# Hybrid mLSTM and DeltaNet layer on one core: which buffers hold the split keys and queries, and which engine transposes and scales in the first segment

## The chip, the core and the metric

The kernel runs on one core of a Trainium2 chip. A core has five engines with an instruction stream of their own, which wait for one another through semaphores: TensorE (PE, matrix products into PSUM), VectorE (DVE), ScalarE (ACT), GpSimd (POOL) and SyncE (SP), whose queue issues nearly all DMAs here. The metric is the device time of one execution in microseconds (us); lower is better.

## The reference, cut to what matters

One layer: an input norm, one joint projection, two families of heads (4 mLSTM heads with 128 key and 256 value columns, 8 gated DeltaNet heads with 128 and 128), a gate on each, an output projection, a final norm. The sequence has 2048 tokens of 1024 columns, all in fp32.

```python
h = rms_norm(x, attn_norm)
mq, mk, mv, mo, mz, mi, mf, gqkv, gz, gb, ga = split(h @ w_in)
# mLSTM, per chunk: D = decay matrix, P = exp(D - m) * (q k^T)
num = w_inter * (q C) + P v
C = decay * C + (ws * k)^T v                  # ws: a weight per token
# gated DeltaNet, per chunk:
a_mat = I + strict_lower((beta k) k^T * gamma)
U, W = triangular_solve(a_mat, [beta v, beta k e^g])
v_new = U - W S ; o = q e^g S + tril(q k^T * gamma) v_new ; S = e^g_last S + k'^T v_new
x = x + concat(y_m, y_g) @ w_out ; out = rms_norm(x, final_norm)
```

## The kernel before

The 2048 tokens are cut into 4 segments of 512; in a segment a chunk is 128 tokens, so each step has 4 chunks. A segment runs eight windows: P0 M0 P1 M1 P2 M2 P3 M3 (in the last segment M2 and M3 stand behind P3). Window P*n* projects DeltaNet pair *n* (two heads, j = 0 and 1): columns `gq`, `gk`, `gv`, `gz`. Window M*n* projects mLSTM head *n*: `mq`, `mk`, `mv`, `mo`, `mz`. Each fp32 product is made of three products of fp32r parts (`hh`, `hl` of the activations, `whi`, `wlo` of the weights). After the segments comes the output projection, from about 1905 us.

Between the projections' matmuls stand the matmuls of the recurrences. The order of TensorE's instructions is written out (`manual_schedule`); the other engines are ordered by a scheduler's own timeline and `high_priority`, and each runs its instructions strictly in its list's order. Work of a pair or head runs in the windows behind its projection: the gate rows and decay matrices of pair *n* in window M*n*, the triangular solve and the chain of products in the next P and M windows, the mLSTM chunks of head *n* in window P*n+1*.

What the change touches:

- **First segment (`raw[0]`).** Here x is projected before it is normalised, because the norm's factor `rbc0` is not ready, and the weights are split on the fly by ACT (L179) and POOL (L182). `fm_out` (L375) therefore multiplies each projected tile by `rbc0` on DVE as it copies it from PSUM: `mq`, `mk`, `xingk` and so on.
- **Keys of an mLSTM head by token.** `mk` comes with tokens along the columns; the state's update needs them along the partitions (`kw`). The table `MT` says for each of three kinds of segment (first, middle two, last) and head which engine transposes: 1 is DVE, 16 transposes of 32x128 (L504, called from L590); 0 is TensorE, four 128x128 transposes by `ident` into a PSUM tile `ktp` (L601), with a copy scaled by `ws` on DVE (L603). Heads marked in `MF` ("fast") make two fp32r parts of `ws*kw` instead, `kws_pt` (ACT, L609) and `kws_nm` (DVE, L610). In the first segment heads 0 to 2 are fast, head 3 is not; its `kw` is scaled by POOL (L595).
- **Split keys and queries of a pair.** `split_kq(j)` (L789) makes `kh` (ACT) and `kl` (DVE and POOL, L804) of head j; the products `kk` (L821 to L823) read them in the order j = 0 then 1, two chunks each. The tiles are borrowed: j = 0 takes two tiles of tag `xk` (which the segment's x rows `xt` and `load_h` also use), j = 1 takes `lbt` (the tile that later holds the solve's matrix, and in other windows the gate rows' `ew` and the split `pts`) and the tiles `pt` and `nm`. There is one tile each of `lbt`, `pt` and `nm`.
- **What uses `nm` next.** The decay rows of the following mLSTM head are loaded into `nm` by a DMA (L561). DVE makes `ptt` from it (L565), ACT its exponential (L567). Behind that ACT copies `mk` (L371, later segments), DVE transposes it into `kw`, and then takes the value tile `vlo` out of PSUM (L537 in the first segment, L540 later). Projections go into three PSUM tiles `pj`, so TensorE stops at a product `pt_mv` (L363) when `vlo` is three tiles late.
- **The solve of a pair.** `ua` (L832) goes to memory and comes back as `lbt` (L841, L845); 31 steps of `tb` and `xb` (L850, L854) follow on DVE, then DMAs `e_d` and `E`, then `dmz` (L904, L905), for which the products `zp` (L910) wait on TensorE.
- **End of a segment.** `rms_stats` of the next one loads its four `xt` tiles (L131), ACT squares them (L132), DVE makes `rs` (L133), POOL its power (L137) and DVE `dg` (L140). `load_h` makes `hl` (L342) of four row tiles, the last of which stands in `lbt`, so it waits for the end of pair 3's solve; the first products of the next segment, `pt_gz` (L363 to L365), need it.

Of the kernel before, what the change touches and what calls it, by code (L numbers as in the profile page):

```python
# [10 lines left out]
F32 = mybir.dt.float32  # L11
F32R = mybir.dt.float32r
AF = mybir.ActivationFunctionType
ALU = mybir.AluOpType
# [3 lines left out]
P = 128  # L18
# [3 lines left out]
NCH = T // P  # L22
# [12 lines left out]
MW, MPR, VPR = ((0.07, 0.85), 200, 200)  # L35
# [20 lines left out]
VT = ((0, 0, 0, 0), (1, 1, 1, 1), (1, 0, 0, 0))  # L56
KTR = ((0, 0, 0, 0), (1, 1, 1, 1), (0, 1, 0, 0))
QT = ((1, 1, 1, 1), (1, 1, 1, 1), (1, 1, 0, 1))
MT = ((1, 1, 1, 1), (1, 1, 1, 1), (1, 1, 1, 0))
KF = ((0, 1, 1, 1), (1, 1, 1, 1), (1, 1, 1, 0))  # L60
MF = ((1, 1, 1, 0), (1, 1, 1, 0), (1, 0, 0, 0))
KE = ('vector', 'gpsimd')
# [7 lines left out]
def hybrid_layer(  # L70
# [16 lines left out]
    nc = tc.nc  # L87
# [14 lines left out]
    sm = wstack.enter_context(tc.tile_pool(name="sm", bufs=2, side="right"))  # L102
    cl = wstack.enter_context(tc.tile_pool(name="cl", bufs=2, side="right"))
    wkp = ctx.enter_context(tc.tile_pool(name="wkp", bufs=1, side="left"))
# [86 lines left out]
    for seg in range(NSEG):  # L191
        for kind, n in ORDER_LAST if seg == NSEG - 1 else ORDER:
            for i in range(4) if kind == "M" else (3, 1, 0, 2) if n == 0 else (1, 0, 2, 3):
                nm, key = f"{kind}{seg}_{n}_{i}", (kind, n, i)
# [40 lines left out]
    rbc0 = cst.tile([P, T], F32, name="rbc0")  # L235
# [131 lines left out]
    def fm_out(dst, ps, scale=None):  # L367

        if not raw[0]:
            if scale is None:  # L370
                nc.scalar.copy(dst, ps)  # L371
            else:
                nc.scalar.activation(dst, ps, AF.Copy, scale=scale)
        elif scale is None:
            nc.vector.tensor_tensor(dst, ps, rbc0, op=ALU.mult)  # L375
        else:
            nc.vector.scalar_tensor_tensor(dst, ps, scale, rbc0, op0=ALU.mult, op1=ALU.mult)

    def tm_done(ps, t, done, scaled=True):
        if raw[0] and scaled:  # L380
# [115 lines left out]
    def by_dve(which, seg, pr):  # L496
        return which[2 if seg == NSEG - 1 else min(seg, 1)][pr]

    def to_tokens(src, dst):

        s4 = src.rearrange("p (c a j) -> p c a j", c=NCH, a=4)
        for a in range(4):
            for b in range(4):
                nc.vector.transpose(dst[32 * a:32 * a + 32, :, 32 * b:32 * b + 32],  # L504
                                    s4[32 * b:32 * b + 32, :, a, :])


    def m_proj(seg, n, r):
# [46 lines left out]
    def m_chunks(seg, h, r, st):  # L555
        s_ = f"{seg}_{h}"
# [3 lines left out]
        nm = wk.tile([P, T], F32, tag="nm", name=f"nm{s_}")  # L560
        nc.sync.dma_start(nm, st["rows"][h, :].partition_broadcast(P))  # L561
        pt = wk.tile([P, T], F32, tag="pt", name=f"ptt{s_}")
# [14 lines left out]
        fast = by_dve(MF, seg, h)  # L577
# [10 lines left out]
            ps2 = split(pt, "pts", wkp, "lbt", nc.vector)  # L588
            qw2 = split(qw, "qws", sm, "xk", nc.gpsimd, bufs=XKB)
        yield  # L590
        kw = sm.tile([P, NCH, P], F32, tag="kw", name=f"kw{s_}", bufs=1)
        if fast or by_dve(MT, seg, h):
            to_tokens(kT, kw)
            if not fast:
                nc.gpsimd.tensor_tensor(  # L595
                    kw, kw, ws[:, :, h:h + 1].broadcast_to([P, NCH, P]), op=ALU.mult)
        else:
            ktp = psc.tile([P, 512], F32, tag="cp", name=f"ktp{s_}")
            for c in range(NCH):
                cs = slice(c * P, (c + 1) * P)  # L600
                nc.tensor.transpose(ktp[:, cs], kT[:, cs], ident)  # L601
            for c in range(NCH):
                nc.vector.tensor_scalar_mul(  # L603
                    kw[:, c, :], ktp[:, c * P:(c + 1) * P], ws[:, c, h:h + 1])
        if fast:
            kw2 = [wk.tile([P, NCH, P], F32R, tag=tag, name=f"kws{s_}_{tag}") for tag in ("pt", "nm")]
            for c in range(NCH):
# [4 lines left out]
                    op0=ALU.mult, op1=ALU.subtract)  # L612
# [124 lines left out]
    def g_prep(seg, pr, r, st):  # L737
        s_ = f"{seg}_{pr}"
# [9 lines left out]
        for j in range(2):  # L748
# [4 lines left out]
            for c in range(NCH):  # L753
                nc.vector.scalar_tensor_tensor(
                    ua_[:, c, 1, :], gbc[:, c * P:(c + 1) * P], gcol[:, c, h0 + j:h0 + j + 1],
                    negmask, op0=ALU.subtract, op1=ALU.min)
# [31 lines left out]

        def split_kq(j):  # L789

            kh = (wkp.tile([P, NCH, 2, P], F32R, tag="lbt", name=f"kh{s_}_{j}") if j else
                  sm.tile([P, NCH, 2, P], F32R, tag="xk", name=f"kh{s_}_{j}", bufs=XKB))
            if j:
                kl = [wk.tile([P, 2, 2, P], F32R, tag=tag, name=f"kl{s_}_{j}_{tag}")
                      for tag in ("pt", "nm")]
            else:
                kl_ = sm.tile([P, NCH, 2, P], F32R, tag="xk", name=f"kl{s_}_{j}", bufs=XKB)
                kl = [kl_[:, 0:2], kl_[:, 2:4]]
            for i, f in enumerate((kT[j], qT[j])):
                f = f.rearrange("p (c t) -> p c t", c=NCH)  # L800
                nc.scalar.copy(kh[:, :, i, :], f)
                for c2 in range(2):
                    cs = slice(c2 * 2, c2 * 2 + 2)
                    getattr(nc, KE[i]).tensor_tensor(  # L804
                        kl[c2][:, :, i, :], f[:, cs], kh[:, cs, i, :].bitcast(F32),
                        op=ALU.subtract)
            return kh, kl

        fast = by_dve(KF, seg, pr)
        kqs = [split_kq(j) for j in range(2)] if fast else None  # L810
        l_d = dpool.tile([2 * NCH, 4, 1024], F32, tag="l_d", name=f"l_d{s_}")
        for j in range(2):
            ua_ = ua[j]
            for c2 in range(NCH // 2):
                kp = psc.tile([P, 512], F32, tag="cp", name=f"kk{s_}_{j}_{c2}").rearrange(
                    "p (a b c) -> p a b c", a=2, b=2)
                for a in range(2):
                    if fast:
                        kh, kl = kqs[j]
# [10 lines left out]
                for a in range(2):  # L830
                    c = c2 * 2 + a
# [6 lines left out]
        lbt = wkp.tile([P, 32, 32], F32, tag="lbt", name=f"lbt{s_}")  # L838
# [43 lines left out]
        if by_dve(QT, seg, pr):  # L882
# [3 lines left out]
            for a in range(4):  # L886
# [4 lines left out]
                                op0=ALU.mult, op1=ALU.add)  # L891
# [209 lines left out]
    for seg in range(NSEG):  # L1101
# [17 lines left out]
        for kind, n in ORDER_LAST if last else ORDER:  # L1119
# [27 lines left out]
            else:  # L1147
# [256 lines left out]
```

## Time and profile before

| what | value |
|---|---|
| runs, us | 2284.42, 2275.52, 2281.76; median 2281.76 |
| the profiled execution | 2285.25 us, its span 2283.5 us |
| TensorE (PE) | busy 2210.1 us, 97% of the span, 14798 matmuls |
| VectorE (DVE) | busy 1842.6 us, 81% |
| ScalarE (ACT), GpSimd (POOL) | 38%, 35% |
| chain that ended last | PE 62%, DVE 25%, DMA 5%, ACT 4% |
| mean granted TensorE clock | 0.985 of full speed |

The span is what the trace covers; the execution's own time is 1.75 us longer. Busy times overlap, so they don't add up to the span. The chain is followed back from the last instruction, at each step to what released it; an engine's share of it says how often the end hung on that engine.

### The profile page before, as it was taken

How to read it: one execution, taken by the hardware profiler on the slowest of the kernel's cores; microseconds unless marked ns; L12 is line 12 of the kernel's file. 1: busy time of each engine (PE TensorE's matmuls, PEld its weight loads, DVE VectorE, ACT ScalarE, POOL GpSimd, SP SyncE). 2: the span in 40 equal slices, each digit the busy share in tenths (PEclk: the TensorE clock that was granted, in tenths of full speed). 3: DMA queues.
4: the chain of work that ended last, by engine and by line, in shares of the span. 5: the costliest groups of instructions: out<-in, count | busy, mean ns of one | idle time of the engine just before them, and what ended most of it. 6: DMA issues, size and time to landing. Idle time of an engine off the chain costs nothing.

```text
span 2283.5 us, 41793 instructions
## 1 busy us (share of the span) xinstructions
PE 2210.1 (97%) x14798; PEld 1963.8 (86%) x14798; DVE 1842.6 (81%) x5168; ACT 861.8 (38%) x2289; POOL 797.3 (35%) x1220
## 2 busy tenths in 40 slices
PE   8899999989999999999999999999999999999998
PEld 7779898987989898988898989898988997788787
DVE  7988888788897979888979798788757737878784
ACT  5445454535343434352424243524244334111111
POOL 4657565652120202521212114212111115555543
PEclk9999999999999999999999999999999999999999
DMA  8767676764536464655454546544546545222321
GB/s 273 265 236 252 231 242 240 255 216 157 193 135 213 138 212 159 224 167 182 162 187 163 176 169 237 178 152 166 184 168 209 192 152 162 80 96 92 102 84 65
DMA packets 183322, 409.19 MB, mean 179 GB/s; under 512 B 51736, under 2 KB 84632, under 8 KB 183112
## 3 DMA queue, kind: packets, MB, share of 16 engines
q1 hardware_dynamic: 182392, 405.74, 52.4%
q8 instruction: 116, 1.90, 0.3%
q14 instruction: 94, 0.77, 0.1%
q10 hardware_dynamic: 720, 0.79, 0.1%
HBM read 309.68 MB, written 96.90 MB: 178 GB/s over the span
## 4 chain that ended last, share of the span: by engine, by line
PE 62%; DVE 25%; DMA 5%; ACT 4%; issue 2%; POOL 2%; SPq 0%; POOLq 0%; ACTq 0%; DVEq 0%
PE po L1260 5%; PE po L1259 5%; PE po L1258 5%; DVE tb L850 3%; DVE xb L854 3%; DVE kw L504 2%; PE pf_gv L355 2%; PE pf_gv L353 2%; PE pf_gv L354 2%; PE pt_gz L365 2%; PE pf_gq L353 2%; PE pt_gz L363 2%; PE pt_gz L364 2%; PE pt_mo L363 2%; PE pt_mo L364 2%
## 5 line engine op out<-in xcount | busy, mean ns | idle before, releaser
L1219 DVE STREAM_TRANSPOSE ytt<-yl 32x256 f32<-32x256 f32 x448 | 195.3, 436 | 45.3 <-POOL ylo L1187 39.2
L1016 POOL TENSOR_TENSOR gms<-gms,nhalf 128x2 f32<-128x2 f32 x64 | 46.7, 729 | 395.8 <-DVE gms L1014 386.5
L850 DVE TENSOR_TENSOR tb<-xb,lbt 128x248 f32<-128x248 f32 (+30 forms) x496 | 170.1, 343 | 17.8 <-DMA lbt<-l_d 5.0
L854 DVE TENSOR_TENSOR xb<-xb,tb 128x248 f32<-128x248 f32 (+30 forms) x496 | 167.7, 338 | 13.2
L363 PE MATMUL pt_mv<-whi_M,hh 128*128 128x256 f32 x512 | 152.7, 298 | 21.7 <-DVE vlo L540 14.6
L363 PE MATMUL pt_mz<-whi_M,hh 128*128 128x256 f32 x512 | 149.7, 292 | 7.6 <-DVE tz L550 7.5
L363 PE MATMUL pt_gz<-whi_P,hh 128*128 128x256 f32 (+1 forms) x512 | 149.7, 292 | 1.8 <-ACT whi_P L179 1.5
L364 PE MATMUL pt_mv<-wlo_M,hh 128*128 128x256 f32 x512 | 148.6, 290 | 0.1
L365 PE MATMUL pt_mv<-whi_M,hl 128*128 128x256 f32 x512 | 148.5, 290 | 0.0
L363 PE MATMUL pt_mo<-whi_M,hh 128*128 128x256 f32 x512 | 148.4, 290 | 0.0
L365 PE MATMUL pt_gz<-whi_P,hl 128*128 128x256 f32 (+1 forms) x512 | 146.7, 286 | 0.4 <-DVE hl L342 0.2
L364 PE MATMUL pt_gz<-wlo_P,hh 128*128 128x256 f32 (+1 forms) x512 | 146.4, 286 | 0.4 <-DVE wlo_P L182 0.4
L365 PE MATMUL pt_mz<-whi_M,hl 128*128 128x256 f32 x512 | 145.1, 283 | 0.0
L364 PE MATMUL pt_mz<-wlo_M,hh 128*128 128x256 f32 x512 | 145.1, 283 | 0.0
L364 PE MATMUL pt_mo<-wlo_M,hh 128*128 128x256 f32 x512 | 144.2, 282 | 0.0
L365 PE MATMUL pt_mo<-whi_M,hl 128*128 128x256 f32 x512 | 144.2, 282 | 0.0
L363 PEld LDWEIGHTS pt_mv<-whi_M,hh 128*128 128x128 f32 x512 | 101.4, 198 | 25.1 <-DVE vlo L540 16.0
L1267 ACT ACTIVATE jkf<-xr 128x512 f32<-128x512 f32 (+1 forms) x33 | 20.4, 619 | 271.5 <-DVE xr L1265 148.4
L1258 PE MATMUL po<-woh,yh 128*128 128x512 f32 (+1 forms) x297 | 114.6, 386 | 1.5 <-ACT yh L1185 1.5
L1260 PE MATMUL po<-woh,ylo 128*128 128x512 f32 (+1 forms) x297 | 114.9, 387 | 0.1
L1259 PE MATMUL po<-wol,yh 128*128 128x512 f32 (+1 forms) x297 | 114.3, 385 | 0.0
L182 POOL TENSOR_TENSOR wlo_M<-wraw_M,whi_M 128x256 fp32r<-128x256 f32 x128 | 98.4, 801 | 40.6 <-ACT whi_M L179 40.6
(407 smaller groups left out, 7541.7 us busy)
## 6 DMA issues: line engine op xcount, KB each, us to landing
whi_M<-wdM SPq DMA_DIRECT2D x96, 512.0 KB, 4.0
wlo_M<-wdM SPq DMA_DIRECT2D x96, 512.0 KB, 5.5
whi_P<-wdP SPq DMA_DIRECT2D x90, 512.0 KB, 4.7
wlo_P<-wdP SPq DMA_DIRECT2D x90, 512.0 KB, 6.0
wraw_M<-in_wg_dram SPq DMA_DIRECT2D x32, 512.0 KB, 5.8
wdM<-whi_M SPq DMA_DIRECT2D x32, 512.0 KB, 2.9
wdM<-wlo_M SPq DMA_DIRECT2D x32, 512.0 KB, 5.0
wraw_P<-in_wg_dram SPq DMA_DIRECT2D x30, 512.0 KB, 5.7
```

The lines of the kernel that those rows point to most:

```text
L182: eng.tensor_tensor(lo[:, ks, :], raw_[:, ks, :], hi[:, ks, :].bitcast(F32), op=ALU.subtract)
L353: nc.tensor.matmul(ps, lhsT=hi[k // HK][:, k % HK, c0:c0 + P], rhs=hh[k], start=(k == 0), stop=False)
L363: nc.tensor.matmul(ps, lhsT=hh[k][:, ts], rhs=hi, start=(k == 0), stop=False)
L364: nc.tensor.matmul(ps, lhsT=hh[k][:, ts], rhs=lo, start=False, stop=False)
L365: nc.tensor.matmul(ps, lhsT=hl[k][:, ts], rhs=hi, start=False, stop=(k == KT - 1))
L850: nc.vector.tensor_tensor(tb[:, :, 0:n], xb[:, :, i:i + 1].broadcast_to([P, 8, n]), lbt[:, i:i + 1, i + 1:32].broadcast_to([P, 8, n]), op= ...
L854: nc.vector.tensor_tensor(xs, xs, tb[:, :, 0:n], op=ALU.subtract)
L1016: nc.gpsimd.tensor_tensor(ms, ms, nhalf[:, 0:2], op=ALU.pow)
L1219: nc.vector.transpose(ytt[32 * b:32 * b + 32, :, 32 * a:32 * a + 32], y3[32 * a:32 * a + 32, :, 32 * b:32 * b + 32])
L1258: nc.tensor.matmul(ps, lhsT=yh, rhs=woh, start=(k == 0), stop=False)
L1259: nc.tensor.matmul(ps, lhsT=yh, rhs=wol, start=False, stop=False)
L1260: nc.tensor.matmul(ps, lhsT=ylo, rhs=woh, start=False, stop=(k == 15))
```

## The change

Three edits. In `split_kq` the heads swap their tiles: j = 0 now takes `lbt` with `nm` (chunks 0 and 1) and `pt` (chunks 2 and 3), and j = 1 takes the two `xk` tiles. In `MT` the first segment's four heads go from 1 to 0; for the fast heads 0 to 2 there is no copy of the transposed keys, `kws_pt` and `kws_nm` read the PSUM tile, and head 3 is scaled by DVE out of PSUM instead of POOL. In `fm_out` of the first segment the product by `rbc0` is issued with a raised priority and as SCALAR_TENSOR_TENSOR with 1.0 instead of TENSOR_TENSOR.

```diff
--- before.py
+++ after.py
@@ -56,7 +56,7 @@
 VT = ((0, 0, 0, 0), (1, 1, 1, 1), (1, 0, 0, 0))
 KTR = ((0, 0, 0, 0), (1, 1, 1, 1), (0, 1, 0, 0))
 QT = ((1, 1, 1, 1), (1, 1, 1, 1), (1, 1, 0, 1))
-MT = ((1, 1, 1, 1), (1, 1, 1, 1), (1, 1, 1, 0))
+MT = ((0, 0, 0, 0), (1, 1, 1, 1), (1, 1, 1, 0))
 KF = ((0, 1, 1, 1), (1, 1, 1, 1), (1, 1, 1, 0))
 MF = ((1, 1, 1, 0), (1, 1, 1, 0), (1, 0, 0, 0))
 KE = ('vector', 'gpsimd')
@@ -371,10 +371,10 @@
                 nc.scalar.copy(dst, ps)
             else:
                 nc.scalar.activation(dst, ps, AF.Copy, scale=scale)
-        elif scale is None:
-            nc.vector.tensor_tensor(dst, ps, rbc0, op=ALU.mult)
         else:
-            nc.vector.scalar_tensor_tensor(dst, ps, scale, rbc0, op0=ALU.mult, op1=ALU.mult)
+            with tc.high_priority(VPR):
+                nc.vector.scalar_tensor_tensor(
+                    dst, ps, 1.0 if scale is None else scale, rbc0, op0=ALU.mult, op1=ALU.mult)
 
     def tm_done(ps, t, done, scaled=True):
         if raw[0] and scaled:
@@ -588,8 +588,9 @@
             ps2 = split(pt, "pts", wkp, "lbt", nc.vector)
             qw2 = split(qw, "qws", sm, "xk", nc.gpsimd, bufs=XKB)
         yield
-        kw = sm.tile([P, NCH, P], F32, tag="kw", name=f"kw{s_}", bufs=1)
-        if fast or by_dve(MT, seg, h):
+        if by_dve(MT, seg, h) or not fast:
+            kw = sm.tile([P, NCH, P], F32, tag="kw", name=f"kw{s_}", bufs=1)
+        if by_dve(MT, seg, h):
             to_tokens(kT, kw)
             if not fast:
                 nc.gpsimd.tensor_tensor(
@@ -599,7 +600,9 @@
             for c in range(NCH):
                 cs = slice(c * P, (c + 1) * P)
                 nc.tensor.transpose(ktp[:, cs], kT[:, cs], ident)
-            for c in range(NCH):
+            if fast:
+                kw = ktp.rearrange("p (c f) -> p c f", c=NCH)
+            for c in range(0 if fast else NCH):
                 nc.vector.tensor_scalar_mul(
                     kw[:, c, :], ktp[:, c * P:(c + 1) * P], ws[:, c, h:h + 1])
         if fast:
@@ -788,11 +791,11 @@
 
         def split_kq(j):
 
-            kh = (wkp.tile([P, NCH, 2, P], F32R, tag="lbt", name=f"kh{s_}_{j}") if j else
+            kh = (wkp.tile([P, NCH, 2, P], F32R, tag="lbt", name=f"kh{s_}_{j}") if not j else
                   sm.tile([P, NCH, 2, P], F32R, tag="xk", name=f"kh{s_}_{j}", bufs=XKB))
-            if j:
+            if not j:
                 kl = [wk.tile([P, 2, 2, P], F32R, tag=tag, name=f"kl{s_}_{j}_{tag}")
-                      for tag in ("pt", "nm")]
+                      for tag in ("nm", "pt")]
             else:
                 kl_ = sm.tile([P, NCH, 2, P], F32R, tag="xk", name=f"kl{s_}_{j}", bufs=XKB)
                 kl = [kl_[:, 0:2], kl_[:, 2:4]]
```

Lines of the changed kernel behind L600 are 3 higher than those of before. TensorE's order changes only by the insertion of four transposes for each of the first segment's heads; DVE has 3510 rows in place of 3500, ACT 1582 for 1571, POOL 784 for 790 and SP 977 for 973.

DVE, first segment, from the evacuation of head 0's keys `mk` to the first value tiles `vlo` (`qs` and `ssq` are sums of squares of the pair's queries, `ua` the decay matrix of the next pair). Before:

```order
L375 TENSOR_TENSOR mk_0_819<-pf_mk_0_913,rbc_175 128x512
L885 TENSOR_TENSOR qs_0_1021<-qs_0_1021 32x32
L504 STREAM_TRANSPOSE kw_0_1622<-mk_0_819 32x4x32 x2
L885 TENSOR_TENSOR qs_0_1021<-qs_0_1021 32x32
L504 STREAM_TRANSPOSE kw_0_1622<-mk_0_819 32x4x32 x7
L885 TENSOR_TENSOR qs_0_1021<-qs_0_1021 32x32
L504 STREAM_TRANSPOSE kw_0_1622<-mk_0_819 32x4x32 x7
L887 COPY ssq_0_847<-qs_0_1021 32x2x4 x4
L537 SCALAR_TENSOR_TENSOR vlo_0_1079<-pt_mv_0_0_1080,rs_173,mv_0_820 128x256
L890 TENSOR_SCALAR cq_0_1051<-ssq_0_847 128x8
L754 SCALAR_TENSOR_TENSOR ua_1_2207<-gbc_1_0_2210,cq_704,negmask 128x128 x4
L754 SCALAR_TENSOR_TENSOR ua_1_2207<-gbc_1_1_2217,cq_704,negmask 128x128
```

After:

```order
L376 SCALAR_TENSOR_TENSOR mk_0_819<-pf_mk_0_913,rbc_175 128x512
L888 TENSOR_TENSOR qs_0_1021<-qs_0_1021 32x32 x3
L890 COPY ssq_0_847<-qs_0_1021 32x2x4 x4
L893 TENSOR_SCALAR cq_0_1051<-ssq_0_847 128x8
L537 SCALAR_TENSOR_TENSOR vlo_0_1079<-pt_mv_0_0_1080,rs_173,mv_0_820 128x256
L757 SCALAR_TENSOR_TENSOR ua_1_2195<-gbc_1_0_2198,cq_704,negmask 128x128 x4
L757 SCALAR_TENSOR_TENSOR ua_1_2195<-gbc_1_1_2205,cq_704,negmask 128x128
L537 SCALAR_TENSOR_TENSOR vlo_0_1079<-pt_mv_0_1_1107,rs_173,mv_0_820 128x256
L757 SCALAR_TENSOR_TENSOR ua_1_2195<-gbc_1_1_2205,cq_704,negmask 128x128 x3
L537 SCALAR_TENSOR_TENSOR vlo_0_1079<-pt_mv_0_2_1134,rs_173,mv_0_820 128x256
L853 TENSOR_TENSOR tb_0_952<-xb_0_830,lbt_0_943 128x8x31
```

The 16 transposes between `mk` and the first `vlo` are gone from DVE; of the rest only `cq` changes place, to ahead of the first `vlo`.

DVE, second segment, pair 1's `ua` and head 1's keys (`ptt` is made from the decay rows in `nm`, `vr` is a value residue of pair 0's chain). Before:

```order
L832 SCALAR_TENSOR_TENSOR ua_1_8202<-kk_1_1_1_8343,scol_1_8256,ua_1_8202 128x256 x2
L885 TENSOR_TENSOR qs_1_8436<-qs_1_8436 32x32 x3
L887 COPY ssq_1_8220<-qs_1_8436 32x2x4 x4
L565 SCALAR_TENSOR_TENSOR ptt_1_8962<-nm_1_8960,ccol_6710,negmask 128x128 x3
L890 TENSOR_SCALAR cq_1_8466<-ssq_1_8220 128x8
L565 SCALAR_TENSOR_TENSOR ptt_1_8962<-nm_1_8960,ccol_6710,negmask 128x128
L504 STREAM_TRANSPOSE kw_1_9045<-mk_1_8192 32x4x32 x12
L976 SCALAR_TENSOR_TENSOR vr_0_2_8231<-sp_0_2_8491,neg_6724,vr_0_2_8231 128x128 x2
L504 STREAM_TRANSPOSE kw_1_9045<-mk_1_8192 32x4x32 x4
L540 TENSOR_TENSOR vlo_1_8477<-pt_mv_1_0_8478,mv_1_8193 128x256
```

After:

```order
L835 SCALAR_TENSOR_TENSOR ua_1_8158<-kk_1_0_1_8271,scol_1_8212,ua_1_8158 128x256 x2
L565 SCALAR_TENSOR_TENSOR ptt_1_8918<-nm_1_8916,ccol_6666,negmask 128x128 x4
L871 TENSOR_REDUCE qs_1_8392<-qtp_1_0_8393 128x16
L1021 SCALAR_TENSOR_TENSOR gyt_0_1_8263<-op_0_1_8255,gms_0_1_8262,gg_0_6030 128x128 x2
L835 SCALAR_TENSOR_TENSOR ua_1_8158<-kk_1_1_0_8284,scol_1_8212,ua_1_8158 128x256 x2
L871 TENSOR_REDUCE qs_1_8392<-qtp_1_1_8405 128x16
L835 SCALAR_TENSOR_TENSOR ua_1_8158<-kk_1_1_1_8299,scol_1_8212,ua_1_8158 128x256 x2
L888 TENSOR_TENSOR qs_1_8392<-qs_1_8392 32x32 x3
L890 COPY ssq_1_8176<-qs_1_8392 32x2x4 x4
L893 TENSOR_SCALAR cq_1_8422<-ssq_1_8176 128x8
L504 STREAM_TRANSPOSE kw_1_9001<-mk_1_8148 32x4x32 x16
L979 SCALAR_TENSOR_TENSOR vr_0_2_8187<-sp_0_2_8447,neg_6680,vr_0_2_8187 128x128 x2
```

`ptt` stands behind the second piece of `ua` instead of behind the fourth and the sums `ssq`; the transposes follow the sums without it between.

DVE at the end of the first segment, where head 3's keys, the start of pair 3's solve (`tb`, `xb`) and the next segment's norm (`rs`, `dg`) meet. Before:

```order
L375 TENSOR_TENSOR mk_3_5199<-pf_mk_3_5346,rbc_175 128x512
L504 STREAM_TRANSPOSE kw_3_5945<-mk_3_5199 32x4x32 x14
L976 SCALAR_TENSOR_TENSOR vr_2_2_5244<-sp_2_2_5549,neg_769,vr_2_2_5244 128x128 x2
L504 STREAM_TRANSPOSE kw_3_5945<-mk_3_5199 32x4x32 x2
L133 TENSOR_SCALAR rs_5471<-rs_5471 128x4
L850 TENSOR_TENSOR tb_3_5389<-xb_3_5210,lbt_3_5380 128x8x31
L854 TENSOR_TENSOR xb_3_5210<-xb_3_5210,tb_3_5389 128x8x31
```

After:

```order
L376 SCALAR_TENSOR_TENSOR mk_3_5163<-pf_mk_3_5310,rbc_175 128x512
L893 TENSOR_SCALAR cq_3_5472<-ssq_3_5191 128x8
L979 SCALAR_TENSOR_TENSOR vr_2_2_5208<-sp_2_2_5513,neg_769,vr_2_2_5208 128x128 x2
L853 TENSOR_TENSOR tb_3_5353<-xb_3_5174,lbt_3_5344 128x8x31
L133 TENSOR_SCALAR rs_5435<-rs_5435 128x4
L857 TENSOR_TENSOR xb_3_5174<-xb_3_5174,tb_3_5353 128x8x31
L853 TENSOR_TENSOR tb_3_5353<-xb_3_5174,lbt_3_5344 128x8x30
L1009 SCALAR_TENSOR_TENSOR SS_255<-SS_255,egl_772,su_2_2_5660 128x128
L857 TENSOR_TENSOR xb_3_5174<-xb_3_5174,tb_3_5353 128x8x30
L1009 SCALAR_TENSOR_TENSOR SS_256<-SS_256,egl_772,su_2_2_5660 128x128
L853 TENSOR_TENSOR tb_3_5353<-xb_3_5174,lbt_3_5344 128x8x29
L140 TENSOR_SCALAR dg_5450<-ident,rs_5435 128x128 x2
```

The transposes are gone, the first solve step stands ahead of `rs`, and work of pair 2's chain (`SS`, `gms`) stands between the solve's steps.

## Rows read from the trace of the kernel before

**Rows 1.** The page, busy time, share of the span and count of each engine.

```profile
PE 2210.1 (97%) x14798; PEld 1963.8 (86%) x14798; DVE 1842.6 (81%) x5168; ACT 861.8 (38%) x2289; POOL 797.3 (35%) x1220
```

**Rows 2.** All waits of PE: engine, line, what for; us, times, longest.

```profile
PE pt_mv L363 <- DVE vlo L540: 14.6, 7, 3.4
PE pt_mz L363 <- DVE tz L550: 7.5, 5, 3.1
PE vq L982 <- DVE vr L976: 4.8, 2, 3.8
...
PE pt_mv L363 <- DVE vlo L537: 3.1, 2, 3.0
PE zp L910 <- DVE dmz L904: 3.0, 2, 1.8
```

**Rows 3.** The same waits, first 690 to 820 us, then 1155 to 1285 us.

```profile
PE pt_mv L363 <- DVE vlo L540: 3.7, 2, 1.9
...
PE pt_mv L363 <- DVE vlo L540: 3.6, 2, 1.9
```

**Rows 4.** Groups by line: L504 to 560 us, the others whole span.

```profile
L504 DVE STREAM_TRANSPOSE kw<-mk 32x128 f32<-32x128 f32 x64 | 19.4, 302 | 1.0
...
L601 PE MATMUL ktp<-ident,mk 128*128 128x128 f32 x4 | 0.6, 273 | 0.0
...
L603 DVE TENSOR_SCALAR kw<-ktp,ws 128x128 f32<-128x128 f32 x4 | 1.1, 344 | 4.1 <-PE ktp L601 4.1
```

**Rows 5.** DVE, first pair's solve: start, duration, instruction, idle before.

```profile
102.09 0.41 DVE L850 TENSOR_TENSOR tb<-xb,lbt 128x248 f32<-128x248 f32 x1
...
134.42 0.18 DVE L854 TENSOR_TENSOR xb<-xb,tb 128x8 f32<-128x8 f32 x1
...
142.99 0.43 DVE L904 STREAM_TRANSPOSE dmz<-E 32x256 f32<-32x256 f32 x1
```

**Rows 6.** Solve steps of that pair on DVE, then POOL at that time.

```profile
114.73 0.32 DVE L850 TENSOR_TENSOR tb<-xb,lbt 128x160 f32<-128x160 f32 x1
115.08 0.74 DVE L854 TENSOR_TENSOR xb<-xb,tb 128x160 f32<-128x160 f32 x1
...
114.72 6.31 POOL L182 TENSOR_TENSOR wlo_P<-wraw_P,whi_P 128x256 fp32r<-128x256 f32 x8 [4.52 <-ACT whi_P L179]
```

**Rows 7.** Stretch, length, busy (x) PE PEld DVE ACT POOL, PEclk, DMA.

```profile
690.00:699.00 9.00, 7.10 (x60) 6.90 (x59) 8.12 (x26) 3.37 (x10) 2.38 (x4) 1.00 0.55 198
1269.00:1284.00 15.00, 13.07 (x99) 12.87 (x98) 12.84 (x40) 4.00 (x13) 1.88 (x3) 0.89 0.59 208
```

**Rows 8.** Second segment, pair 1 and head 1: PE, SP's queue, DVE.

```profile
675.11 0.28 PE L823 MATMUL kk<-kh,kl 128*128 128x256 f32 x1
...
682.40 0.40 SPq L561 DMA_DIRECT2D nm<-rows  x1
...
688.20 0.88 DVE L565 SCALAR_TENSOR_TENSOR ptt<-nm,ccol,negmask 128x128 f32<-128x128 f32 x3 [3.19 <-DMA nm<-rows]
...
690.51 3.78 DVE L504 STREAM_TRANSPOSE kw<-mk 32x128 f32<-32x128 f32 x12 [1.09 <-ACT mk L371]
...
696.23 0.76 DVE L540 TENSOR_TENSOR vlo<-pt_mv,mv 128x256 fp32r<-128x256 f32 x2
```

**Rows 9.** End of the first segment: DVE, then PE.

```profile
445.48 4.41 DVE L504 STREAM_TRANSPOSE kw<-mk 32x128 f32<-32x128 f32 x14
...
487.49 0.17 DVE L854 TENSOR_TENSOR xb<-xb,tb 128x8 f32<-128x8 f32 x1
...
498.17 0.68 DVE L342 TENSOR_TENSOR hl<-xk,hh 128x512 fp32r<-128x512 f32 x1
...
505.10 0.29 PE L365 MATMUL pt_gz<-whi_P,hl 128*128 128x280 f32 x1
```

**Rows 10.** End of the second segment: DVE, then PE.

```profile
923.03 0.88 DVE L140 TENSOR_SCALAR dg<-ident,rs 128x128 f32<-128x128 f32 x4 [1.93 <-POOL rs L137]
...
968.87 0.40 PE L365 MATMUL pt_gz<-whi_P,hl 128*128 128x280 f32 x1 [0.20 <-DVE hl L342]
```

## The prediction

> **What bounds the kernel now.** I read the page first. TensorE is busy for 2210.1 us, 97% of the span [rows 1], so in all some 70 of 2283.5 us can be won without taking matmuls away, and any DVE work that no matmul waits for is worth nothing. DVE is second, with 81%. So the next view is the list of TensorE's waits [rows 2]. The reader is to see there that the waits are many, short, and nearly all on DVE: 14.6 us in 7 waits for `vlo` of the middle and last segments, 7.5 us in 5 for `tz`, 4.8 us in 2 for `vr`, 3.1 and 3.0 us in the first segment for `vlo` and `dmz`. These five rows make 33.0 us, and are the pool from which the change can draw.
>
> The same list cut to two stretches [rows 3] shows which of the seven belong to heads 1 and 2 of the second and third segments: two and two, 3.7 and 3.6 us. A stall has a second price, the clock: the stretch around the stall at 1275 us has a granted clock of 0.89 over 15 us, that around the stall at 696 us, of 1.90 us, has 1.00 [rows 7]. So a stall of about 2 us sometimes costs 15 x 0.11 = 1.7 us more and sometimes nothing. [...]
>
> Then I read in time the places where these stalls arise, DVE beside SP's queue and TensorE. For head 1 of the second segment [rows 8]: the first chunk's products of the pair end at 675.39, but the load of `nm` is issued only at 682.40, since `nm` holds keys of the pair's last chunk. DVE stands 3.19 us for that load, does `ptt` at 688.20, waits 1.09 more for ACT's `mk`, which is queued behind the exponential of `nm`, and starts the transposes at 690.51. The first `vlo` follows at 696.23, and TensorE has been standing for it.
>
> **Part 1: the buffers, second and third segment.** With j = 0 in `nm`, its last reader is the product that ended at 675.39 in place of the one just ahead of the load's issue, so the load can be issued some 7 us earlier. It takes up to 5.8 us from its issue to `ptt` [rows 8]: 681.2 then, and the new DVE order has a place for `ptt` there. ACT's `mk` no longer waits for the exponential, and the transposes can start when the matmuls of `mk` are done, at about 686.5, so 4 us earlier than now. The 1.90 us stall is covered. The same holds for the other three of its kind [rows 3]: -3.7 and -3.6 us, and -1.7 us of clock at 1275 [rows 7], together **-9.0** (bounds: 0, if the wait is only replaced, and -10.7, if one more stall had its clock dropped). The split itself is not late: j = 0's tiles are read first, but the list of waits has none of a `kk` product for either head's split, and their order on TensorE stays.
>
> What stands behind: in SP's queue the `nm` load moves ahead of both gate rows' loads, and one of these now stands ahead of the loads of weights and of `l_d`. `lbt` arrives a little later by that, so the solve starts no earlier than before. I cost this at 0, because the solve's result is wanted a window later.
>
> **Part 2: transposes of the first segment.** DVE loses 64 transposes of 302 ns, 19.4 us, 4.8 us a head [rows 4]. TensorE gains four transposes a head, 0.6 us busy for four, 2.4 us in all [rows 4]. For head 0 all 4.8 us lie ahead of the first `vlo`; the wait of 3.0 us [rows 2] vanishes. But this does not shorten the program by 3: the next thing that TensorE needs is `dmz`, for which it stands 3.0 us in two waits [rows 2]. Its chain runs from the first solve step at 102.09 over 62 steps to 134.42, two DMAs, and `dmz` at 142.99 [rows 5]. The solve's first step stands in DVE's order behind the third `vlo`, whose product TensorE must first make; I work this start out as 2.1 us earlier rather than 4.8. So head 0 gives **-2.1** (bounds 0 and -4.8).
>
> For heads 1 and 2 the freed DVE time shortens small waits, each shorter than those listed in rows 2; against it stand the transposes on TensorE. I set the two off against each other: **0** (bounds +2.4, all transposes and no gain, and -3.0, as much as the `dmz` waits of rows 2). Head 3 also moves its scaling from POOL to DVE, 4 x 344 ns = 1.4 us. The one place where the same four run now has DVE wait 4.1 us for the transposes [rows 4]; I take 0 for this, since the scheduled place is in the midst of the solve, well behind the transposes, and keep +4.1 for the range of the next part. The raised priority of `fm_out` and the other opcode move nothing that I can price: the tile is the same, one pass over 128x512; 0.
>
> **Part 3: end of the first segment.** Here TensorE's waits for `vr` (up to 3.8 us) and `tz` (3.1 us) [rows 2] lie at 477 and 486 us. DVE loses the 4.8 us of transposes from 445.48 on [rows 9] and the wait ahead of them, so these stalls should go: up to -7.9 us. But the order puts work that ran behind the solve (the state's update, `gms`, mLSTM gates) between its steps. Adding their durations up row by row I get some 9.2 us ahead of the solve's last step, which was at 487.49 [rows 9]. Its end frees `lbt`, into which the fourth row tile of the next segment is loaded; `hl` of it ran at 498.17 and TensorE reads it at 505.10, 6.2 us after its end at 498.85 [rows 9]. 9.2 - 4.8 = 4.4 us later would still fit under 6.2, but `rs` now stands between the first two steps of the solve and must wait for ACT's squares of x rows, whose load waits for the last product of j = 1 in `xk` and no longer for j = 0; some 3 to 5 us more. Then TensorE, arriving up to 8 us earlier, waits for `hl` and resumes 1 to 3 us later than now, with a dropped clock behind it. I take **+3** (bounds -5 and +7: the stalls vanish and nothing replaces them but 3 us; all of 9.2 + 4 less the 6.2 of cover).
>
> **Part 4: ends of the second and third segments.** The same move of `xt` behind j = 1 holds. There `hl` is already just in time, TensorE waited 0.20 us [rows 10]. `dg` waited 1.93 us for POOL's `rs` and the solve stands behind it [rows 10]; if the squares come later by the 6 us between the products, the solve starts some 1 to 2.5 us later, and each us of it is one of TensorE's. I take +1.5 each, **+3** (bounds 0 and +5; a gain isn't excluded where the `tz` waits of rows 2 vanish, -3.5).
>
> **Part 5: first heads and the last segment.** Their `vlo` waits make 14.6 - 7.3 = 7.3 us in three [rows 2, 3]. Window P1's loads are less affected, because pair 0's chain precedes; a few tenths each, **-1.2** (0 to -4).
>
> **Sum.** -9.0 - 2.1 + 0 + 3 + 3 - 1.2 = -6.3 us. The profiled execution took 2285.25, so it would take 2279.0; it lies 3.5 above the median of the runs, 2281.76, on which I put the forecast: **2275.5**. What a measurement of this kernel can tell from no change is about 0.5%, 11.4 us.
>
> [...] Solve steps take 0.32 us alone and 0.74 us from the moment at which POOL splits weights, of which one burst takes 6.31 us [rows 6]. [...]
>
> **Rivals.**
> A. *All DVE stalls of the stretch go.* For it: each is short, and DVE is relieved by 19.4 us in the first segment. Of the 33.0 us about half, with some clock, and no new waits at the segment ends: -18, **2264**. Against it: `hl` and `dmz` are next in line. Chance 0.24.
> B. *The solve at the segments' ends is late and decides, on the other side.* For it: 0.20 us of cover at 968.87, 9.2 us of inserted work at the first end. If `hl` is 9 us late at the first (net of 6.2 and 8 of vanished stalls) and 4 at the other two, +17 - 11.2 = +5.8, **2287.6**. It decides from the point at which the three delays beyond cover exceed 11 us in sum. Chance 0.2, of which 0.09 beyond 0.5%.
> C. *The solve's gain is eaten by POOL.* One burst of 6.31 us covers 8 steps, 8 x 0.42 = 3.4 us: head 0 gives +1.3 in place of -2.1, **2278.8**. Chance 0.08.
> D. *The load of `nm` comes no earlier* because SP's queue or `rows` holds it: parts 1 and 5 at 0, **2286**. Against it: the queue stood idle ahead of 681.5. Chance 0.05.
>
> The forecast's own case has 0.43. Its own range, from -1 to -11, is 2271 to 2281. The range for all reaches to A's and B's prices: 2262 to 2288. Faster by over the bound: A, and a little of the first, 0.28; slower: 0.1; within: 0.62.
>
> **What would show it.** Part 1: DVE's waits at `ptt` for `nm` (3.19 us here) gone, no `vlo` wait of TensorE in 690 to 820 and 1155 to 1285, clock 1.00 there. Part 2: no `vlo` wait near 97, while `mk`'s stall ahead of it stays, and a `dmz` wait of some 3 us or more near 140. Part 3: no waits at 477 and 486, one of `pt_gz` on `hl` near 495 to 507. Part 4: `pt_gz` on `hl` of 1 to 2.5 us at 965 and its like a segment later. The prediction is wrong if the waits at the segments' ends sum to over 11 us, or if they do not appear.

## The result, and the profile after

The changed kernel takes 2301.65 us (median of 4 runs, 2297.9 to 2301.96), the kernel before 2283.09 us (4 runs): ratio 1.0071, with an interval of 1.0055 to 1.0086. By the ratio it is slower by some 16 us (the medians lie 18.6 apart) where I forecast 6 us faster. The profiled execution has a span of 2300.0 us, 16.5 more than before.

The page of the changed kernel, first part, the row that answers to [rows 1]:

```profile
PE 2215.6 (96%) x14814; PEld 1971.1 (86%) x14814; DVE 1830.9 (80%) x5108; ACT 864.4 (38%) x2289; POOL 799.7 (35%) x1219
```

DVE has 11.7 us less work and TensorE is busy 5.5 us longer, at a mean clock of 0.981 for 0.985; the span has grown by three times as much. So two thirds of the time are in waits. The largest waits of TensorE in the changed kernel (us in total, times, longest), the answer to [rows 2]; lines behind L600 are 3 higher than before, and L375 is L376:

```profile
PE zq L933 <- DVE dmz L928: 9.9, 6, 3.8
PE zp L913 <- DVE dmz L907: 9.4, 4, 5.7
PE pt_gz L363 <- ACT hh L341: 8.6, 3, 3.8
PE rbp L145 <- DVE dg L140: 7.6, 3, 4.9
PE pt_mv L363 <- DVE mk L376: 6.9, 4, 3.5
...
PE pt_mv L363 <- DVE vlo L540: 4.6, 2, 3.0
PE pt_mz L363 <- DVE tz L550: 4.4, 4, 2.0
```

The reader is to see both sides in it. The waits for `vlo` fell from 14.6 us in 7 to 4.6 in 2, those for `vr` are gone. In their place stand waits for the results of the solves (`dmz`, 19.3 us with `zq` and `zp`; `zp` alone was 3.0) and for the next segment's rows (`hh`, 8.6, and `dg`, 7.6), which the list of before does not have above a microsecond.

Where did it happen? Both traces have the same matmuls in the same order but for the new transposes, so the start of one and the same matmul can be compared. Changed less before, in us, from TensorE's rows in time (each from one execution; that of before took 2.2 us more than its median):

| matmul | before | changed | difference |
|---|---|---|---|
| first `pf_gk` of segment 2 | 509.43 | 511.36 | +1.9 |
| first `pt_mo` of its head 2 | 813.37 | 811.37 | -2.0 |
| first `pf_gk` of segment 3 | 973.23 | 978.35 | +5.1 |
| first `pt_mo` of its head 2 | 1280.14 | 1275.77 | -4.4 |
| first `pf_gk` of segment 4 | 1439.75 | 1443.53 | +3.8 |
| first `pf_gv` of its pair 2 | 1684.45 | 1686.56 | +2.1 |
| first `pt_mo` of its head 2 | 1801.72 | 1819.27 | +17.6 |

It is a saw: heads 0 to 2 of a middle segment win 3.9 and 9.5 us, each end of a middle segment loses 7.1 and 8.2, and one stretch of the last segment loses 15.4.

The wins are those of part 1. The changed kernel's windows (columns as in [rows 7]) at the two stretches of that group, shifted with the program:

```profile
690.00:699.00 9.00, 9.00 (x79) 9.00 (x78) 5.62 (x19) 2.40 (x7) 1.43 (x2) 1.00 0.86 295
1264.00:1279.00 15.00, 15.00 (x130) 15.00 (x129) 10.01 (x36) 3.52 (x11) 1.43 (x2) 1.00 0.82 267
```

TensorE is busy throughout and the clock is 1.00 in both. SP's queue and then DVE at head 1 of the second segment, the answer to [rows 8]:

```profile
677.83 0.37 SPq L561 DMA_DIRECT2D nm<-rows  x1
683.87 0.32 SPq L753 DMA_DIRECT2D gbc<-rows  x1
...
694.89 2.36 SPq L848 DMA_DIRECT2D lbt<-l_d  x4
```

```profile
682.14 2.59 DVE L565 SCALAR_TENSOR_TENSOR ptt<-nm,ccol,negmask 128x128 f32<-128x128 f32 x4
...
689.50 5.04 DVE L504 STREAM_TRANSPOSE kw<-mk 32x128 f32<-32x128 f32 x16
...
695.09 0.74 DVE L540 TENSOR_TENSOR vlo<-pt_mv,mv 128x256 fp32r<-128x256 f32 x2
```

The load of `nm` is issued at 677.83 in place of 682.40, `ptt` runs 6 us earlier, with no wait, and the transposes in one piece.

The end of the second segment, DVE, then TensorE, then the window behind it, the answer to [rows 10]:

```profile
923.87 0.17 DVE L133 TENSOR_SCALAR rs<-rs 128x4 f32<-128x4 f32 x1 [3.70 <-ACT xt L132]
924.04 0.42 DVE L853 TENSOR_TENSOR tb<-xb,lbt 128x248 f32<-128x248 f32 x1
```

```profile
970.72 0.60 PE L363 MATMUL pt_gz<-whi_P,hh 128*128 128x280 f32 x1 [2.15 <-ACT hh L341]
```

```profile
970.00:976.00 6.00, 5.07 (x20) 4.74 (x21) 3.45 (x12) 1.52 (x3) 2.49 (x6) 0.55 0.18 41
```

DVE stands 3.70 us at `rs` for ACT's squares of the x rows, and the solve behind it. Before, `rs` ran without such a wait:

```profile
920.93 0.17 DVE L133 TENSOR_SCALAR rs<-rs 128x4 f32<-128x4 f32 x1
```

The solve's last step is at 962.38 in place of 959.76, on a program that was 2.0 us ahead. `hh` of the last rows is late by 2.15 us, and from 970 to 976 the clock is 0.55, where it was 1.00 from 960 to 970: some 6 x 0.45 = 2.7 us more, an estimate.

The last segment, where most went. DVE before, pair 2's first and last solve step, the first and the last `dmz`:

```profile
1741.05 0.41 DVE L850 TENSOR_TENSOR tb<-xb,lbt 128x248 f32<-128x248 f32 x1
...
1774.75 0.17 DVE L854 TENSOR_TENSOR xb<-xb,tb 128x8 f32<-128x8 f32 x1
...
1780.27 0.43 DVE L904 STREAM_TRANSPOSE dmz<-E 32x256 f32<-32x256 f32 x1 [1.23 <-DMA E<-e_d]
...
1781.37 0.44 DVE L904 STREAM_TRANSPOSE dmz<-E 32x256 f32<-32x256 f32 x1
```

TensorE then, without a wait:

```profile
1782.68 0.69 PE L910 MATMUL zp<-dmz,ua 32*32 32x32 f32 x32
```

The same of the changed kernel (its first `dmz`), then pair 3's first solve step and `dmz` of the next product `zq`, then TensorE's stalls and two windows behind them:

```profile
1746.65 0.42 DVE L853 TENSOR_TENSOR tb<-xb,lbt 128x248 f32<-128x248 f32 x1 [1.08 <-DMA lbt<-l_d]
...
1784.57 0.18 DVE L857 TENSOR_TENSOR xb<-xb,tb 128x8 f32<-128x8 f32 x1
...
1790.04 0.43 DVE L907 STREAM_TRANSPOSE dmz<-E 32x256 f32<-32x256 f32 x1 [4.51 <-DMA E<-e_d]
...
1797.59 0.42 DVE L853 TENSOR_TENSOR tb<-xb,lbt 128x248 f32<-128x248 f32 x1 [3.86 <-DMA lbt<-l_d]
...
1800.09 3.15 DVE L504 STREAM_TRANSPOSE kw<-mk 32x128 f32<-32x128 f32 x10
1803.27 0.43 DVE L928 STREAM_TRANSPOSE dmz<-E 32x256 f32<-32x256 f32 x1
```

```profile
1790.62 0.28 PE L913 MATMUL zp<-dmz,ua 32*32 32x32 f32 x2 [5.74 <-DVE dmz L907]
1791.46 1.06 PE L913 MATMUL zp<-dmz,ua 32*32 32x32 f32 x30 [0.56 <-DVE dmz L907]
...
1803.76 1.54 PE L933 MATMUL zq<-dmz,ua 64*64 64x64 f32 x12 [3.77 <-DVE dmz L928]
```

```profile
1790.00:1797.00 7.00, 5.82 (x67) 4.33 (x69) 3.38 (x12) 1.03 (x3) 0.00 (x0) 0.53 0.66 178
1803.00:1810.00 7.00, 6.24 (x36) 5.90 (x37) 6.51 (x16) 0.95 (x2) 1.27 (x1) 0.53 0.00 0
```

The solve starts 5.6 us later, of which 2.1 are the program's shift at that place, and ends 9.8 later: pair 3's `ktok` and `ua`, which stood behind the solve's last step in the kernel before, now lie between its last eight instructions. `zp` stands 5.74 us for it. Then DVE stands 3.86 us for pair 3's `lbt`, whose first solve step its list now has ahead of `kw`'s transposes (before, it ran behind them, at 1794.08); these stand ahead of `dmz`, and `zq` stands 3.77 more. The three stalls make 10.1 us. In the two windows behind them the clock is 0.53, which on 12.1 busy us costs some 5.7, an estimate; together that is about the 15.4 lost.

### The profile page after: what moved, and what is told of

It reads as the page before. It is cut to its first block, busy times and chain, and to the rows that moved or that the text cites. A ratio compares the mean times of both kernels' runs of the same rounds, so it can differ in the third digit from the quotient of the medians.

```text
span 2300.0 us, 41784 instructions
## 1 busy us (share of the span) xinstructions
PE 2215.6 (96%) x14814; PEld 1971.1 (86%) x14814; DVE 1830.9 (80%) x5108; ACT 864.4 (38%) x2289; POOL 799.7 (35%) x1219
## 4 chain that ended last, share of the span: by engine, by line
PE 62%; DVE 24%; DMA 5%; ACT 3%; issue 2%; POOL 2%; SPq 1%; POOLq 0%; DVEq 0%; ACTq 0%
PE po L1263 5%; PE po L1261 5%; PE po L1262 5%; DVE xb L857 3%; DVE tb L853 3%; PE pt_gz L365 2%; PE pt_gz L363 2%; PE pt_gz L364 2%; DVE ktok L504 2%; PE pf_gv L355 2%; PE pf_gv L353 2%; PE pf_gv L354 2%; DVE gv L504 2%; PE pt_mo L363 2%; PE pt_mo L364 2%
```

## The experiments

All ratios are to the kernel before, run on the same chip, with an interval of 95%. Where a table `SW` is used, it is added to the changed kernel; 1 means the changed kernel's buffers and 0 those of before, for the pairs 0 to 3 of the first, the middle two and the last segment. Its line numbers are then 1 higher than the changed kernel's, behind L793 2 higher (4 in `e8` and `e12`). An edit is cut at each `...`:

```diff
+SW = ((0, 0, 0, 0), (1, 1, 1, 0), (0, 0, 0, 0))
...
-            kh = (wkp.tile([P, NCH, 2, P], F32R, tag="lbt", name=f"kh{s_}_{j}") if not j else
+            low = j == (0 if by_dve(SW, seg, pr) else 1)
+            kh = (wkp.tile([P, NCH, 2, P], F32R, tag="lbt", name=f"kh{s_}_{j}") if low else
...
-            if not j:
+            if low:
                 kl = [wk.tile([P, 2, 2, P], F32R, tag=tag, name=f"kl{s_}_{j}_{tag}")
-                      for tag in ("nm", "pt")]
+                      for tag in (("nm", "pt") if by_dve(SW, seg, pr) else ("pt", "nm"))]
```

**Which edit.** `e1_swap_only` has the change's edit of `split_kq` and nothing else of it; against the kernel before:

```diff
-            kh = (wkp.tile([P, NCH, 2, P], F32R, tag="lbt", name=f"kh{s_}_{j}") if j else
+            kh = (wkp.tile([P, NCH, 2, P], F32R, tag="lbt", name=f"kh{s_}_{j}") if not j else
...
-            if j:
+            if not j:
...
-                      for tag in ("pt", "nm")]
+                      for tag in ("nm", "pt")]
```

> Only the buffers change places; first segment's keys and fm_out as before. Theory S (the swap costs time: in the last segment the early ptt pushes ua, the solve of pair 2 ends 9.8 us later and zp and zq stand; and at segment ends the x rows load later): 2295 to 2303 us, zp and zq waits near 1790 as in the changed kernel. Rival F (the first segment's edits cost the time, by another order that drifts on): 2272 to 2283 us, no such waits.

Measured: 2302.43 us, 1.0094 (1.0071 to 1.0116). `e2_no_swap` is the opposite, `MT` and `fm_out` changed and the buffers as before; against the kernel before, without the lines that go with `MT` and those of `fm_out`:

```diff
-MT = ((1, 1, 1, 1), (1, 1, 1, 1), (1, 1, 1, 0))
+MT = ((0, 0, 0, 0), (1, 1, 1, 1), (1, 1, 1, 0))
```

> Both first-segment edits, buffers as before. Theory S: 2276 to 2284 us, waits from 560 us on as before. Rival F: 2295 to 2303 us.

Measured: 2276.97 us, 0.9968 (0.9956 to 0.9981). The loss is the swap's; the first segment's edits win a third of a percent. Rival F falls.

**Which place.** `e3_swap_not_last`: the changed kernel with

```diff
+SW = ((1, 1, 1, 1), (1, 1, 1, 1), (0, 0, 0, 0))
```

> The changed kernel, but in the last segment the buffers are as before. Theory S with the last segment as its main place: 15 us less than the changed kernel, 2284 to 2289 us, no zp or zq wait near 1790. Rival L (the last segment stands because the kernel comes into it in another state, not because of the swap there): 2297 to 2302 us.

Measured: 2282.46 us, 0.9993 (0.9981 to 1.0005), 0.8% less than the changed kernel, and no `zp` or `zq` wait in it is longer than 1.8 us: the last segment's loss is that of the swap there, and rival L falls. `e4_swap_p012` leaves pair 3 out too:

```diff
+SW = ((1, 1, 1, 0), (1, 1, 1, 0), (0, 0, 0, 0))
```

> The changed kernel, but pair 3 of every segment and all of the last segment with the buffers as before, so that x rows of the next segment load as early as before. Theory S: the vlo waits of heads 1 and 2 stay away and the segment ends lose their extra waits, 2268 to 2277 us. Rival H (the ends stand because TensorE arrives earlier, whatever the buffers): the gain is given back at hl, 2280 to 2286 us.

Measured: 2268.74 us, 0.9933 (0.9917 to 0.9949). In its list of waits there is none for `hh` or `dg` over a microsecond; rival H falls: TensorE comes to the segments' ends earlier than in the changed kernel, and does not stand there.

**Within the last segment.** `e5_last_pair2` and `e6_last_pairs01` add the swap of one or two pairs of it to e4:

```diff
+SW = ((1, 1, 1, 0), (1, 1, 1, 0), (0, 0, 1, 0))
...
+SW = ((1, 1, 1, 0), (1, 1, 1, 0), (1, 1, 0, 0))
```

> The kernel of e4 (2268.7 us), and the swap in pair 2 of the last segment too. If pair 2 alone makes the last segment's loss: 2280 to 2286 us, with zp and zq waits on dmz of some 6 and 4 us near the end of that segment. If the loss needs the swap of the pairs ahead of it too: 2267 to 2273 us.

> The kernel of e4, and the swap in pairs 0 and 1 of the last segment. If pair 2 alone makes the loss: 2265 to 2271 us. Otherwise 2280 to 2286 us.

Measured: 0.9997 (0.9985 to 1.0009) for pair 2, 0.9935 (0.9912 to 0.9957) for pairs 0 and 1. Pair 2 alone makes the loss, 0.64%. The two longest sums of TensorE's waits for `dmz` in e5:

```profile
PE zp L915 <- DVE dmz L909: 10.5, 4, 6.0
...
PE zq L935 <- DVE dmz L930: 8.9, 6, 2.7
```

`e8_last_pair2_lbt_early` takes the swap of that pair apart, so that `kh` alone takes the other tile, `nm` and `pt` keep their late release, and one `xk` tile comes free late in place of two; against e4:

```diff
+            lkh = j == 0 if (seg == NSEG - 1 and pr == 2) else low
+            low = j == 1 if (seg == NSEG - 1 and pr == 2) else low
-            kh = (wkp.tile([P, NCH, 2, P], F32R, tag="lbt", name=f"kh{s_}_{j}") if low else
+            kh = (wkp.tile([P, NCH, 2, P], F32R, tag="lbt", name=f"kh{s_}_{j}") if lkh else
```

> As e5, but of pair 2 in the last segment only kh and the xk tiles change places: j = 0 has kh in lbt and kl in xk, j = 1 has kh in xk and kl in pt and nm, so lbt comes free early and nm as late as before. If the early nm (its ptt and the order that follows) makes the loss: 2266 to 2272 us as e4. If the early lbt or the late xk makes it: 2280 to 2286 us as expected of e5.

Measured: 0.9922 (0.9897 to 0.9946), no loss against e4. So in this place it is neither the early `lbt` nor one late `xk` tile, but the early `nm`, with `pt`, into which `ptt` is written. e5 has the second `xk` tile late too; that this does no harm is read from the traces alone: the last load of output weights, which goes into such a tile, is issued some 46 us behind pair 2's first `pf_gv` in both, and in e8 `l_d` is not late. In e5 and in the changed kernel `ptt` stands between the second and third piece of `ua`, and ahead of `l_d` SP's queue has two loads of the output weights and one of `whi_P`; in e4 and e8 `ptt` follows `ua`, and the queue has `l_d` ahead of that weight. Counted from the same `pf_gv`, the last piece of `ua` comes 1.0 us later in the changed kernel than before, `l_d` 1.7, `lbt` 3.4 and the first solve step 3.5, and the solve then takes 4.2 us longer for what lies between its steps; 3.5, 4.2 and the shift of 2.1 make the 9.8 us. No run took these pieces apart.

**The segments' ends.** `e7_pair3` is e2 with the swap in pair 3 alone, which keeps the `vlo` waits:

```diff
+SW = ((0, 0, 0, 1), (0, 0, 0, 1), (0, 0, 0, 0))
```

> The kernel of e2 (first-segment edits, 2277.0 us), and the swap in pair 3 of the first three segments only. If the segment ends stand because the x rows load behind j = 1: 2285 to 2292 us, with waits for dg and hh at each end. If the ends stand in the changed kernel only because TensorE comes there earlier (the vlo waits ahead of them are not away here): 2275 to 2280 us.

Measured: 2294.46 us, 1.0031 (1.0019 to 1.0044), 0.63% more than e2, with these waits of TensorE:

```profile
PE pt_mv L364 <- DVE vlo L541: 14.5, 7, 3.3
PE pt_gz L364 <- ACT hh L342: 9.3, 3, 3.9
PE rbp L146 <- DVE dg L141: 8.9, 3, 5.3
```

The ends stand without TensorE being early. `e12_pair3_lbt_early` does with pair 3 what e8 did with pair 2 (`lkh` for `seg < NSEG - 1 and pr == 3`): `nm` late as before, one of the two `xk` tiles free after j = 0, the other after j = 1.

> As e7, but in pair 3 j = 0 has kh in lbt and kl in xk, j = 1 has kh in xk and kl in pt and nm: nm comes free as late as before, and one of the two xk tiles late. If the early nm makes the loss at the segment ends too: as e2, a ratio to before of 0.996 to 0.999. If the late load of the x rows makes it: half of e7's loss or more is left, 1.000 to 1.004.

Measured: 1.0020 (1.0009 to 1.0032). Of e7's loss against e2 some five sixths (0.52 of 0.63%) are left, so here it is not mainly `nm`; the waits are 6.0 us for `hh` and 13.7 for `tz`. It is the late `xk` or the early `lbt`. The waits of `rs` for ACT's squares speak for the first: at the end of the second segment none before, 3.71 us in e7 and, with one late tile, 1.92 in e12:

```profile
918.27 0.17 DVE L134 TENSOR_SCALAR rs<-rs 128x4 f32<-128x4 f32 x1 [1.92 <-ACT xt L133]
```

The first two loads of x rows follow head 2's first `pt_mo` there by 92.1 and 92.5 us in e2, by 92.1 and 95.6 in e12, by 97.5 and 97.9 in e7 and in the changed kernel. A kernel that frees `lbt` late and `xk` late was not tried.

**The first segment.** In e4 the first segment is slower than in e2 by 5.8 us at its end (first `pf_gk` of the second segment, 504.57 and 498.75). DVE in e4, first segment, `ptt` of head 1:

```profile
200.25 0.35 DVE L566 SCALAR_TENSOR_TENSOR ptt<-nm,ccol,negmask 128x128 f32<-128x128 f32 x1 [3.97 <-DMA nm<-rows]
...
210.47 0.69 DVE L377 SCALAR_TENSOR_TENSOR mk<-pf_mk,rbc 128x512 f32<-128x512 f32 x1
```

Here `ptt` was placed early in the list, but the load was not there: DVE stood 3.97 us, and `ua`, the sums and `mk` (210.47) stood behind it. `e9_middle_p012` therefore swaps only in the middle segments:

```diff
+SW = ((0, 0, 0, 0), (1, 1, 1, 0), (0, 0, 0, 0))
```

> Both first-segment edits, and the swap in pairs 0 to 2 of the second and third segments alone. In e4 the place in the first segment at which head 1 is projected was 4 to 5 us later than in e2, and the second and third segments won some 15 us. If the swap in the first segment is what costs there (ptt stands ahead of ua and waits for nm): 2261 to 2267 us on the scale of e4's 2268.7, a ratio to before of 0.988 to 0.991. If not: as e4, 0.992 to 0.995.

Measured: 2264.91 us, 0.9909 (0.9882 to 0.9935). The profiled span is 2259.7 us, 3.7 below e4's. It beats the kernel before and the changed one. Against e4 the 0.24% lie inside the intervals; but that `pf_gk` comes at 498.5 to 499.5 us in the traces of e2, e9 and e10, which have the transposes on TensorE and no swap in the first segment, and at 504.6 to 507.9 in those of e4, e5, e6 and e8, which swap pairs 0 to 2 there. The two first-segment edits are undone one by one on e9, in `e10_middle_no_fm` and `e11_middle_no_mt`:

> As e9 with fm_out as before. If the raised priority carries nothing: equal to e9 within 0.2%. If it carries the first segment's gain: 5 to 8 us slower than e9.

> As e9 with the first segment's transposes on DVE as before. If these carry the first segment's gain: 6 to 10 us slower than e9. If not: within 0.2% of e9.

Measured: 0.9910 (0.9888 to 0.9932) without the change of `fm_out`, 0.9942 (0.9922 to 0.9963) without the change of `MT`. The priority carries nothing that these runs show; the transposes on TensorE carry 0.33%, 7.5 us (2273.1 to 2274.6 us in e11, 2261.4 to 2271.8 in e9).

Three times lie outside what was expected of the case that they speak for: e3 1.5 us below, e6 2.2 and e7 2.5 above.

Differences to before at the same matmuls, each from one profiled execution, show the pieces side by side (us). These executions lie 3.5 and 3.4 us below their medians in e4 and e9 and 1.5 above in e5:

| kernel | `pf_gk` seg. 2 | `pt_mo` seg. 2 | `pf_gk` seg. 3 | `pt_mo` seg. 3 | `pf_gk` seg. 4 | `pt_mo` seg. 4 |
|---|---|---|---|---|---|---|
| changed | +1.9 | -2.0 | +5.1 | -4.4 | +3.8 | +17.6 |
| e2 no swap | -10.7 | -9.0 | -8.6 | -10.6 | -6.4 | -7.3 |
| e7 pair 3 | -8.3 | -5.4 | +2.6 | +1.9 | +10.6 | +11.8 |
| e4 pairs 0 to 2, not last | -4.9 | -10.0 | -10.0 | -20.2 | -17.9 | -20.2 |
| e5 and pair 2 of the last | -1.6 | -4.7 | -4.3 | -14.2 | -11.7 | +1.1 |
| e9 middle segments | -9.9 | -13.6 | -13.6 | -23.7 | -21.5 | -23.5 |

From e2 to e9 the swap wins 4.7 us by head 2 of the second segment and 13.0 in all by that of the third. e5 comes 6.2 us later into segment 4 than e4 does, though the buffers are the same until there: 3.3 of it are there at the end of the first segment, and since the two executions lie 5.0 us apart in their places among their own runs, little of it is shown to be the kernels'. e5 loses another 15.1 by head 2 of segment 4.

## Why the prediction was wrong

**Part 1, the covered stalls: right, and large enough.** The four `vlo` waits of [rows 3] are gone, the load came 4.6 us earlier on a program that was 2.2 us later (6.8 in all, some 7 were forecast), and the clock stays at 1.00. I counted -9.0; in the stretches between the segments' ends the changed kernel wins 3.9 and 9.5 us, part of which is the first head's `vlo` of part 5 (14.6 us in 7 before, 4.6 in 2 now). The split is not late, as forecast; but a `kk` product of the second segment's first pair now waits 2.7 us at 567.85 for DVE's `SS`, about as long as `sp` had waited there for `ua` before (2.4 us).

**Part 1, "I cost this at 0, because the solve's result is wanted a window later": this step failed.** It is true for a middle segment, where no wait for `dmz` grew: before, the last `dmz` of a pair's first product was ready 7.8 to 15.7 us ahead of `zp` in most copies of the chain behind the first, 2.2 to 2.8 at pair 0 of the second to fourth segments. In the last segment P3 follows P2 at once, with M2 behind it, and there the solve of pair 2 had almost no cover: in the kernel before the last `dmz` ended at 1781.81 and TensorE took it up at 1782.68, 0.87 us later, the smallest lead of all that had one. I looked at the cover in one segment and carried it to all. With the load of `nm` the order of DVE and of SP's queue changed, the solve started late, the next pair's work slid between its last steps, and 15.4 us went in that one stretch; e5 gives 0.64% to that pair alone. None of my rivals had this place.

**Part 4, the ends of the middle segments: mis-sized; the mechanism, late x rows, is borne out by the traces but not shown alone.** I took +1.5 each (up to +5 for both); 7.1 and 8.2 were measured. I counted a delay of the solve's start; the wait for `hh` is 2.15 and 3.8 us, and behind the two stalls the clock was 0.55 (970 to 976) and 0.72 (1436 to 1442), by the estimate above 2.7 us in the first, which I had not added here though I had for a stall that was removed.

**Part 3, the end of the first segment: place wrong, and the size right by luck.** From 453 us to 509.43 the changed kernel loses 2.6 us, +3 was predicted. The wait for `vr` (3.8 us) is gone and 0.6 of 3.1 us is left of that for `tz`, but the new wait that I had put at `hl` came first as 4.94 us at `rbp` for `dg`, [rows 10]'s kind of place, and only then as 2.7 at `hh`.

**Part 2, the first segment's transposes: right in kind, too small.** I put 4.8 us a head on one side and -2.1 in sum, with heads 1 and 2 at nothing. e11 against e9 makes it 7.5 us; in e2 TensorE is 4.4 us ahead once pair 0's solve is used (`pf_gv` of pair 1, 160.93 and 156.50) and 7.6 at head 3's `pt_mo` (453.27 and 445.70). In the changed kernel most of this is not to be seen, since the swap in the first segment takes it back (e2 to e4: 5.8 us).

**The rivals.** B, on the other side, was the nearest: late solves at the segments' ends, 2287.6. Its late ends are shown by e7, and its +17 for the three is near what was measured (2.6, 7.1 and 8.2), but the last segment decides the size. The 11.2 us of gain in it is no sum of the parts: the gains in the sum add up to 12.3, which makes B 2286.5. C: pair 0's solve did start 2.1 us earlier in e2 (99.95 for 102.09 [rows 5]), and `dmz` came 1.8 earlier (141.18); the last four instructions took 0.60 to 0.66 us each, in place of 0.17 to 0.18, while the steps ahead of them took 1.7 us less than before. So of the 2.1 us 0.3 net were eaten, not 3.4. In the changed kernel's trace two instructions of the same solve that ran within a burst of POOL (2.85 us from 127.49) took 0.62 and 0.64 us, in place of 0.20 and 0.19 before, with POOL idle. A and D fall: the load did come earlier, and the other stalls did not all go.

The range of 2262 to 2288 ended where the forecast places ended. What I should have done with rows of before is to ask for each solve, in each segment, how long ahead of its product `dmz` is ready, and price a delay of the solve by the smallest of these, not by the one that I had read.

## What to carry to other kernels

A buffer that is freed earlier does not only remove a wait: the scheduler can move the consumer of that buffer up in its engine's list, and whatever it now stands ahead of is late, as in e4, where DVE stood 3.97 us at `ptt` for `nm` with `ua`, the sums and `mk` behind it. Swap buffers by segment and pair, not everywhere: here 1.0071 for all pairs, 0.9909 for six of them with the same first-segment edits. When two tiles change hands, ask who waited for each of them before, for both (`nm` came early, but the next segment's x rows came late for it), and look at the tightest copy of a repeated chain, which is the one in the irregular last segment.

## What the runs showed of the hardware that was not expected

TensorE stood 2.15 us until 970.72, and from 970 to 976 its mean clock was 0.55; around the stall of 1.90 us in [rows 7] it was 1.00. In these traces the price of a stall of about two microseconds thus varied between nothing and, by the estimate of 2.7 us above, more than the stall itself.
